# Residual written into the down projection's banks by ScalarE, in the FFNs of a four-FFN encoder trunk

## The chip, the core and the metric

The kernel runs on one NeuronCore of one Trainium2 chip. The metric is the device time of one execution in microseconds. Three runs of the kernel before took 912.9, 914.19 and 914.21 us; the median is 914.19.

## The reference

Two macaron layers over 256 tokens of width 1024, in float32. Each has an FFN, a mixer and a second FFN, and each of the three is followed by a layernorm over a scaled residual (DeepNorm). Here `ALPHA` is (2*2)^0.25, about 1.414, and `D_FF` is 2816.

```python
def swiglu(x, w_in, w_out):
    gu = x @ w_in
    g, u = gu[..., :D_FF], gu[..., D_FF:]
    return (jax.nn.silu(g) * u) @ w_out

for l in range(DEPTH):                       # DEPTH = 2
    x = layer_norm(ALPHA * x + 0.5 * swiglu(x, ffn_w_in[l, 0], ffn_w_out[l, 0]), ln_g[l, 0], ln_b[l, 0])
    y = mlstm_mixer(...) if l == 0 else window_attention(...)
    x = layer_norm(ALPHA * x + y, ln_g[l, 1], ln_b[l, 1])
    x = layer_norm(ALPHA * x + 0.5 * swiglu(x, ffn_w_in[l, 1], ffn_w_out[l, 1]), ln_g[l, 2], ln_b[l, 2])
```

A layernorm does not change if its input and the square root of its epsilon are scaled alike, so the kernel normalises 2*ALPHA*x + swiglu(x) with an epsilon four times as large.

## The kernel before

There are six stages, in this order: FFN, mLSTM, FFN, FFN, attention, FFN. They are numbered 0 to 5 in the code; the four FFNs are called FFN 1 to FFN 4 below. The 256 tokens are two tiles (t = 0, 1) of 128 tokens, kept as rows in `xt[t]` (128 x 1024) in SBUF.

**Products.** Every product of float32 numbers is three products of rounded parts (`mm3`, L617): high by high, high by low, low by high. The parts of a weight, `w_hi` and `w_lo`, are made on the chip from the loaded weight: ScalarE makes the high part by a copy of 128 x 1024, and VectorE makes the low part by a subtraction. They live in rings of ten buffers. `Weights` (L189) holds the plan of these splits.

**The order of the work.** The order on each engine's queue is the order in which the program issues it; each engine works its queue strictly in that order. Within an FFN a planner (`Paced`, L65, and `Weights.fill`, L376) decides after each issued matmul whether ScalarE and VectorE get another split now. It keeps estimates of when each engine is free: `on_tensor` (L162) adds n / 2.4 + 13.3 ns for a matmul with n columns and 109 ns for a transpose, and `on_scalar` (L157) adds 0.912 ns a column and 25 ns for an instruction. A split goes in as long as ScalarE's estimate isn't more than 300 ns ahead of TensorE's.

**An FFN.** The first 512 columns of gate and up run first; a narrow unit of 256 columns of gate and of up comes next (L1008 to L1030), and the rest is done in four blocks of 512 columns, each with seven products in place of eight (`seven`, L946). These need sums of pieces of the transposed x, `S1` to `S4`, which VectorE makes from the banks in which x was transposed (`x_sum`, L845) and which ScalarE and VectorE split in two parts (`S_hi`, `S_lo`). The hidden rows are transposed into `hT`, and the down projection follows in steps of 128 hidden columns: `down(n)` (L914) does n such steps, between the products of the next columns. The first step stands right after the narrow unit, whose two Silu (`sg`, one per token tile) and two products `hh` are issued just ahead of it:

```python
for t in range(2):
    sg = temp("sg")[:, 0:256]
    nc.scalar.activation(sg, ps[t][:, 0:256], AF.Silu)
    hh.append(temp("hh")[:, 0:256])
    nc.vector.tensor_mul(hh[t], sg, ps[t][:, 256:512])
...
down(1)
```

**The banks.** PSUM is used as two rings of four banks of 128 x 512: `pw` (`wbank`) for the products on the way, and `py` (`ybank`). The four `py` banks of an FFN are y[t][o], token tile t and half o of the 1024 output columns; they are taken at the first `down` and gather all 22 steps. Before that, the same ring holds the transposed x from which `S1` to `S4` are made.

**The tail and the layernorm.** The last six steps are done by `tail` (L716): tile 0 first, then tile 1, so that the layernorm of tile 0 lies beside the matmuls of tile 1, and that of tile 1 beside the next stage. `Norm.half` (L679) adds the scaled residual on VectorE, x <- alpha*x + y, and takes the statistics of x; `finish` (L695) makes mean and factor (the power on GpSimd), then x <- (x - mean) * g and x <- x * factor + b. `emit_x` (L766) transposes the finished x for the next stage. In the last FFN the second half of tile 1 is split: `first` (L684) adds a first part of its sum early, and two quarters of 256 columns (`quarter`, L689) are added at the very end; there the two passes of the layernorm are done in halves of 512 columns, and each half goes out by a transfer of its own.

Of the kernel before, what the change touches and what calls it, by code (L numbers as in the profile page):

```python
# [16 lines left out]
D = 1024  # L17
S = 256
DEPTH = 2
ALPHA = (2 * DEPTH) ** 0.25  # L20
LN_EPS = 1e-5
# [43 lines left out]
class Paced:  # L65
# [94 lines left out]
            self.mark(o, self.act + 125)  # L160

    def on_tensor(self, name, n, out, ins):  # L162
        self.pe = max(self.pe, self.when(*ins)) + (109.0 if name == "transpose" else n / 2.4 + 13.3)
        for o in out:
            self.mark(o, self.pe + 200)
        if self.filler is not None:
            self.filler()
# [277 lines left out]
def trunk_kernel(ctx: ExitStack, tc: tile.TileContext, x, ffn_w_in, ffn_w_out, ln_g, ln_b, ml_w_in, ml_gate_b,  # L445
                 ml_norm_g, ml_w_out, at_w_in, at_sink, at_w_out, out):
    nc = Paced(tc.nc)
# [126 lines left out]
    xt = [state.tile([128, D], F32, name=f"x{t}", tag=f"x{t}") for t in range(2)]  # L574
# [18 lines left out]
    ident = consts.tile([128, 128], F32, name="ident")  # L593
# [3 lines left out]
    mhalf = consts.tile([128, 2], F32, name="mhalf")  # L597
    nc.gpsimd.memset(mhalf, -0.5)

    gcol = consts.tile([128, 8], F32, name="gcol")  # L600
    gw = consts.tile([128, 8, 16], F32, name="gw")
    gbias = consts.tile([128, 1], F32, name="gbias")
# [14 lines left out]
    def mm3(o, l, r, start, stop, onto=False):  # L617
        nc.tensor.matmul(o, l[0], r[0], start=start, stop=False, skip_group_check=onto)
        nc.tensor.matmul(o, l[0], r[1], start=False, stop=False, skip_group_check=onto)
        nc.tensor.matmul(o, l[1], r[0], start=False, stop=stop, skip_group_check=onto)  # L620

    def pair(p, *idx):
        return p[0][idx], p[1][idx]
# [4 lines left out]
    def ybank(shape=(128, 512)):  # L628
        return psum.tile(list(shape), F32, name="py", tag="py", bufs=4)

    A = slice(None)

    def tok(t):
        return slice(t * 128, (t + 1) * 128)
# [15 lines left out]
    def to_xT(t, src, bank, halves=range(2), high=None):  # L650
        for h in halves:
            p = bank((128, 4, 128))
            for k in range(4):
                nc.tensor.transpose(p[:, k], src[:, (4 * h + k) * 128:(4 * h + k + 1) * 128], ident)
            split_evac(pair(xT, A, slice(4 * h, 4 * h + 4), tok(t)), p, high=high)
            turned[t, h] = p

    def warm(n):

        p = ybank((128, 4, 128))  # L660
        for j in range(n):
            nc.tensor.transpose(p[:, j % 4], ident, ident)

    def load_ln(room, l, n):
        t = []
# [7 lines left out]
    class Norm:  # L673
        def __init__(self, t, ca, eps, gb, last=False):
            self.t, self.ca, self.eps, self.gb, self.last = t, ca, eps, gb, last
            self.stats = state.tile([128, 44], F32, name="stats", tag="stats", bufs=2)[:, 0:18].rearrange("p (h s) -> p h s", h=3)
            self.parts = 2

        def half(self, h, y):  # L679
            z = xt[self.t][:, h * 512:(h + 1) * 512]  # L680
            nc.vector.scalar_tensor_tensor(z, z, self.ca, y, op0=OP.mult, op1=OP.add)
            nc.vector.bn_stats(self.stats[:, h], z)

        def first(self, h, y):  # L684

            z = xt[self.t][:, h * 512:(h + 1) * 512]
            nc.vector.scalar_tensor_tensor(z, z, self.ca, y, op0=OP.mult, op1=OP.add)

# [6 lines left out]
        def finish(self, spare):  # L695
            mv = state.tile([128, 2], F32, name="mv", tag="mv", bufs=2)
            nc.vector.bn_aggr(mv, self.stats[:, 0:self.parts])
            rs = state.tile([128, 2], F32, name="rs", tag="rs", bufs=2)
            nc.vector.tensor_scalar(rs[:, 0:1], mv[:, 1:2], self.eps, None, op0=OP.add)
            nc.gpsimd.tensor_tensor(rs[:, 1:2], rs[:, 0:1], mhalf[:, 0:1], op=OP.pow)  # L700
            z = xt[self.t]
            cuts = [slice(0, 512), slice(512, D)] if self.last or self.t and LC[bound[0]] else [A]
            for s_ in cuts:
                nc.vector.scalar_tensor_tensor(z[:, s_], z[:, s_], mv[:, 0:1], self.gb[0][:, s_],
                                               op0=OP.subtract, op1=OP.mult)
            if len(cuts) == 1:
                W.done(0, spare)
            for s_ in cuts:
                nc.vector.scalar_tensor_tensor(z[:, s_], z[:, s_], rs[:, 1:2], self.gb[1][:, s_],
                                               op0=OP.mult, op1=OP.add)  # L710
                if self.last:
                    nc.sync.dma_start(out[0, tok(self.t), s_], z[:, s_])
            if len(cuts) > 1:
                W.done(0, spare)

    def tail(y, h, todo, first, norm, last, turn_at, between=None, rooms_=None):  # L716

        def one(t, o, n):
            c, (i, w) = todo[t][n]
            end = n == len(todo[t]) - 1 or last and t == o == 1 and n == len(todo[t]) // 2 - 1  # L720
            mm3(y[t][o], h(c, t), pair(w, A, 0, slice(o * 512, o * 512 + 512)), first and n == 0, end)

        full = len(todo[0])
        cut = full - BACK[bound[0]]
        for o, ns in ((0, range(cut)), (1, range(cut)), (0, range(cut, full)), (1, range(cut, full))):
            for n in ns:
                if between is not None and o == 1 and n == turn_at:
                    between()
                one(0, o, n)
                if W.landed:  # L730
                    W.done(0, 0)
            if ns.stop == full and cut < full or cut == full and ns.start == 0:
                norm[0].half(o, y[0][o])
        norm[0].finish(0)
        full = len(todo[1])
        half = full // 2
        order = [(1, n) for n in range(half)] + [(0, n) for n in range(full)] + [(1, n) for n in range(half, full)]
        more = iter(RS[8 * bound[0]:8 * bound[0] + 8])
        for j, (o, n) in enumerate(order):
            if j == full + turn_at:  # L740
                emit_x(0, last)
            if last and j == full + half:
                break
            one(1, o, n)
            if last and j == half - 1:
                norm[1].first(1, y[1][1])
            if j >= half and (n < half) == (o == 0):
                W.done(todo[1][n][1][0] + 1, next(more))
            if n == full - 1:
                norm[1].half(o, y[1][o])  # L750
        if last:
            for q in range(2):
                yq = wbank((128, 256))
                for n in range(half, full):
                    c, (i, w) = todo[1][n]
                    mm3(yq, h(c, 1), pair(w, A, 0, slice(512 + 256 * q, 768 + 256 * q)), n == half, n == full - 1)
                norm[1].quarter(1, q, yq)
        norm[1].finish(1)
        if rooms_ is not None:
            norm[0].gb.clear()  # L760
            W.back(rooms_, 2)
        W.done(most=TD[bound[0]])
        W.owed, W.landed = 0, False
        return lambda: emit_x(1, last)
# [5 lines left out]
    def ffn(l, i, n, pending, last):  # L770
        with ExitStack() as ph:
# [10 lines left out]
            start = pending is None  # L782
# [7 lines left out]
            def tr(hB, t, h):  # L790
                p = wbank((128, 4, 128))
                for k in range(4):
                    nc.tensor.transpose(p[:, k], h[:, k * 128:(k + 1) * 128], ident)
                split_evac(pair(hB, A, A, tok(t)), p, wait=True)

            def chunks(hB, n_):
# [115 lines left out]
            y = []  # L912

            def down(n_):  # L914
                if not y:
                    y.extend([ybank() for _ in range(2)] for _ in range(2))
                W.flush()
                for _ in range(n_):
                    c = done_[0]
                    w, = W.take(1)  # L920
                    for t in range(2):
                        for o in range(2):
                            mm3(y[t][o], pair(hT[c], A, tok(t)), pair(w, A, 0, slice(o * 512, o * 512 + 512)),
                                c == 0, False)
                    W.done()
                    done_[0] += 1

# [105 lines left out]
            def turn():  # L1033
                p = wbank((128, 2, S))
                for t in range(2):
                    for k in range(2):
                        nc.tensor.transpose(p[:, k, tok(t)], hh[t][:, k * 128:(k + 1) * 128], ident)
                split_evac(hp, p, wait=True)

            down(1)  # L1040
# [4 lines left out]
            W.flush()  # L1045
            nc.filler = None
            W.landed = True
            norm = [Norm(t, 2 * ALPHA, 4 * LN_EPS, gb, last) for t in range(2)]
            todo = list(zip(range(2 * UNITS - 6, 2 * UNITS), W.take_rows(6)))
            W.done(0)  # L1050
            return tail(y, lambda c, t: pair(hT[c], A, tok(t)), (todo, todo), False, norm,
# [584 lines left out]
```

## Time and profile before

| | |
|---|---|
| runs | 912.9, 914.19, 914.21 us (median 914.19) |
| profiled execution, from first to last instruction (span) | 911.7 us |
| median over span (what lies around it) | 2.5 us |
| TensorE busy, matmuls | 902.5 us (99%) |
| VectorE busy | 804.4 us (88%) |
| ScalarE busy | 573.1 us (63%) |
| GpSimd busy | 152.5 us (17%) |
| mean granted TensorE clock | 0.999 |

The page gives no time of the profiled execution beside its span. PE is TensorE's matmuls, PEld its weight loads, DVE is VectorE, ACT is ScalarE, POOL is GpSimd. A matmul row has the start and the duration of one matmul, and neighbours overlap because they are pipelined. In a row in order of time the first two numbers are start and duration in microseconds, then come engine, line, operation, written tile <- read tiles, shapes and count, and in brackets how long the engine was idle before it and what ended that. In a row of a group the numbers behind the bar are busy time in microseconds, the mean of one in nanoseconds, and the engine's idle time before them. Nearly all compute instructions have L180 as their line, since a helper issues them; tile names tell them apart: `py` is a bank of y (or of a transposed x), `sg` a Silu, `S_hi` a part of an x sum, `stats` the layernorm's statistics.

### The profile page before, as it was taken

To read this page: it belongs to the slowest core of one execution; us is meant where nothing else is said; L and a number is where in the kernel's file an instruction comes from. 1 tells how busy PE (TensorE), PEld (TensorE's weight loads), DVE (VectorE), ACT (ScalarE), POOL (GpSimd) and SP (SyncE) were. 2 spreads that over 40 slices of the span, in tenths; PEclk is the share of its full clock that TensorE was granted. 3 is DMA by queue.
4 is the path that set the end of the run, shared out by engine and by line. 5 is a ranking of instruction groups with operands and counts; after the bars stand their busy time and mean duration, and the time that the engine had idled before them with its cause. 6 is when DMAs were issued, how large, how long until landed. Compare 5 with 4: busy or idle time off the path is not lost.

```text
span 911.7 us, 12563 instructions
## 1 busy us (share of the span) xinstructions
PE 902.5 (99%) x4459; PEld 757.4 (83%) x4459; DVE 804.4 (88%) x971; ACT 573.1 (63%) x793; POOL 152.5 (17%) x192
## 2 busy tenths in 40 slices
PE   9999999999999999999999999999999999999996
PEld 7888888889988888888888888888898888888885
DVE  5999999886799898999888899998869889899886
ACT  5776777356664656776646676764569566676660
POOL 0111123113211011212011111110425301111110
PEclk9999999999999999999999999999999999999999
DMA  8999998546637898997868989986534587899851
GB/s 281 367 328 259 288 274 215 162 137 186 208 111 246 296 234 244 290 285 234 241 193 269 259 257 283 272 223 197 159 119 140 163 293 221 204 298 278 252 138 47
DMA packets 100703, 208.53 MB, mean 229 GB/s; under 512 B 6904, under 2 KB 21264, under 8 KB 100640
## 3 DMA queue, kind: packets, MB, share of 16 engines
q1 hardware_dynamic: 82368, 173.04, 54.2%
q0 software_dynamic: 17696, 33.65, 22.3%
q10 hardware_dynamic: 576, 1.05, 0.3%
q8 instruction: 35, 0.57, 0.3%
q14 instruction: 28, 0.23, 0.1%
HBM read 206.65 MB, written 1.05 MB: 228 GB/s over the span
## 4 chain that ended last, share of the span: by engine, by line
PE 98%; DVE 1%; DMA 0%; issue 0%; DVEq 0%
PE pw L180 64%; PE py L180 35%; DMA x<-in_x_dram 0%; DVE x L180 0%; DVE stats L180 0%; DVEq L1632 0%; DVE mv L180 0%; DVE rs L180 0%
## 5 line engine op out<-in xcount | busy, mean ns | idle before, releaser
L180 DVE TENSOR_TENSOR w_lo<-w_raw,w_hi 128x1024 fp32r<-128x1024 f32 (+1 forms) x213 | 255.2, 1219 | 26.6 <-ACT w_hi L180 24.8
L180 ACT CAST w_hi<-w_raw 128x1024 fp32r<-128x1024 f32 (+1 forms) x213 | 218.9, 1049 | 80.3 <-PE py L180 21.7
L180 DVE TENSOR_TENSOR w_lo<-s_raw,w_hi 128x1024 fp32r<-128x1024 f32 x192 | 228.6, 1219 | 18.3 <-ACT w_hi L180 18.2
L180 ACT CAST w_hi<-s_raw 128x1024 fp32r<-128x1024 f32 x192 | 196.6, 1054 | 58.4 <-PE py L180 23.3
L180 PE MATMUL pw<-w_hi,xT_hi 128*128 128x512 f32 x480 | 189.5, 396 | 0.0
L180 PE MATMUL pw<-w_hi,xT_lo 128*128 128x512 f32 x480 | 187.0, 391 | 0.0
L180 PE MATMUL pw<-w_lo,xT_hi 128*128 128x512 f32 x480 | 186.7, 390 | 0.0
L122 POOL DMA_DIRECT2D s_raw<-in_ffn_w_in_dram x64 | 77.4, 1211 | 484.1 <-DVE s_raw L180 226.3
L180 PE MATMUL py<-w_hi,h_hi 128*128 128x512 f32 x349 | 138.2, 396 | 0.0
L180 PE MATMUL py<-w_hi,h_lo 128*128 128x512 f32 x349 | 136.2, 390 | 0.0
L180 PE MATMUL py<-w_lo,h_hi 128*128 128x512 f32 x349 | 136.0, 390 | 0.0
L180 PEld LDWEIGHTS pw<-w_hi,xT_lo 128*128 128x128 f32 x480 | 90.0, 188 | 19.1
L180 PEld LDWEIGHTS pw<-w_lo,xT_hi 128*128 128x128 f32 x480 | 90.3, 188 | 18.6 <-DVE w_lo L180 1.2
L180 PEld LDWEIGHTS pw<-w_hi,xT_hi 128*128 128x128 f32 x480 | 90.1, 188 | 17.4 <-ACT w_hi L180 0.2
L180 PE MATMUL pw<-w_hi,S_hi 128*128 128x512 f32 x256 | 99.7, 390 | 0.0
L180 PE MATMUL pw<-w_lo,S_hi 128*128 128x512 f32 x256 | 99.7, 389 | 0.0
L180 PE MATMUL pw<-w_hi,S_lo 128*128 128x512 f32 x256 | 99.7, 389 | 0.0
L180 PEld LDWEIGHTS py<-w_hi,h_lo 128*128 128x128 f32 x349 | 65.5, 188 | 14.1
L180 DVE TENSOR_TENSOR s_raw<-s_raw,s_raw 128x1024 f32<-128x1024 f32 x64 | 76.8, 1219 | 0.3
L180 PEld LDWEIGHTS py<-w_lo,h_hi 128*128 128x128 f32 x349 | 65.7, 188 | 13.0
L180 PEld LDWEIGHTS py<-w_hi,h_hi 128*128 128x128 f32 x349 | 65.6, 188 | 12.7
L180 PEld LDWEIGHTS pw<-w_hi,S_lo 128*128 128x128 f32 x256 | 48.1, 188 | 10.0
(205 smaller groups left out, 1122.7 us busy)
## 6 DMA issues: line engine op xcount, KB each, us to landing
s_raw<-in_ffn_w_in_dram SPq DMA_DIRECT2D x96, 512.0 KB, 8.0
w_raw<-in_ffn_w_out_dram SPq DMA_DIRECT2D x88, 512.0 KB, 6.1
w_raw<-in_ffn_w_in_dram SPq DMA_DIRECT2D x64, 512.0 KB, 5.7
s_raw<-in_ffn_w_in_dram POOLq DMA_DIRECT2D x64, 512.0 KB, 8.3
w_raw<-in_ml_w_in_dram SPq DMA_DIRECT2D x24, 512.0 KB, 4.6
w_raw<-in_ffn_w_in_dram SPq DMA_DIRECT2D x32, 256.0 KB, 6.0
w_raw<-in_at_w_in_dram SPq DMA_DIRECT2D x12, 512.0 KB, 4.8
w_raw<-in_ml_w_out_dram SPq DMA_DIRECT2D x8, 512.0 KB, 4.1
```

The lines of the kernel that those rows point to most:

```text
L122: self.nc.gpsimd.dma_start(ap, source, accum_op=OP.add)
L180: r = f(out, *args, **kw)
```

## The change

In the FFNs, and only there, the scaled residual is added in PSUM. When `down` takes the four y banks, ScalarE writes 2*ALPHA*x into each (four instructions of 128 x 512 per FFN), and all matmuls of the down projection add to what is there: the first step no longer starts a sum. `Norm` is made without a factor for these stages: `half` takes the statistics straight from the bank, `first` copies the early part of the last half-row from its bank to x on ScalarE, and the first pass of `finish` reads the banks, in two halves of 512 columns. The mLSTM and the attention keep the old path.

[...]

```diff
     def on_tensor(self, name, n, out, ins):
-        self.pe = max(self.pe, self.when(*ins)) + (109.0 if name == "transpose" else n / 2.4 + 13.3)
+        self.pe = max(self.pe, self.when(*ins)) + (109.0 if n == 128 else n / 2.4 + 13.3)
...
+    def turn_in(o, a, k):
+        nc.tensor.matmul(o, a, ident, is_transpose=True, start=k == 0, stop=True, skip_group_check=k > 0)
...
+            self.y = {} if ca is None else None
 
         def half(self, h, y):
+            if self.y is not None:
+                nc.vector.bn_stats(self.stats[:, h], y)
+                self.y[h] = y
+                return
...
         def first(self, h, y):
 
+            if self.y is not None:
+                nc.scalar.copy(xt[self.t][:, h * 512:(h + 1) * 512], y)
+                self.y[h] = None
+                return
...
-            for s_ in cuts:
-                nc.vector.scalar_tensor_tensor(z[:, s_], z[:, s_], mv[:, 0:1], self.gb[0][:, s_],
+            for s_ in cuts if self.y is None else [slice(0, 512), slice(512, D)]:
+                y = None if self.y is None else self.y[s_.start // 512]
+                nc.vector.scalar_tensor_tensor(z[:, s_], z[:, s_] if y is None else y, mv[:, 0:1], self.gb[0][:, s_],
                                                op0=OP.subtract, op1=OP.mult)
...
             def down(n_):
                 if not y:
                     y.extend([ybank() for _ in range(2)] for _ in range(2))
+                    for t in range(2):
+                        for o in range(2):
+                            nc.scalar.mul(y[t][o], xt[t][:, o * 512:o * 512 + 512], 2 * ALPHA)
                 W.flush()
...
                             mm3(y[t][o], pair(hT[c], A, tok(t)), pair(w, A, 0, slice(o * 512, o * 512 + 512)),
-                                c == 0, False)
+                                False, False, True)
...
-            norm = [Norm(t, 2 * ALPHA, 4 * LN_EPS, gb, last) for t in range(2)]
+            norm = [Norm(t, None, 4 * LN_EPS, gb, last) for t in range(2)]
```

More of the change, by code (lines that the diff above doesn't have):

```diff
@@ L653, in to_xT @@
             for k in range(4):
-                nc.tensor.transpose(p[:, k], src[:, (4 * h + k) * 128:(4 * h + k + 1) * 128], ident)
+                turn_in(p[:, k], src[:, (4 * h + k) * 128:(4 * h + k + 1) * 128], k)
             split_evac(pair(xT, A, slice(4 * h, 4 * h + 4), tok(t)), p, high=high)
@@ L661, in warm @@
         for j in range(n):
-            nc.tensor.transpose(p[:, j % 4], ident, ident)
+            turn_in(p[:, j % 4], ident, j % 4)
     def load_ln(room, l, n):
@@ L720, in one @@
             end = n == len(todo[t]) - 1 or last and t == o == 1 and n == len(todo[t]) // 2 - 1
-            mm3(y[t][o], h(c, t), pair(w, A, 0, slice(o * 512, o * 512 + 512)), first and n == 0, end)
+            mm3(y[t][o], h(c, t), pair(w, A, 0, slice(o * 512, o * 512 + 512)), first and n == 0, end,
+                norm[0].y is not None)
         full = len(todo[0])
@@ L792, in tr @@
                 for k in range(4):
-                    nc.tensor.transpose(p[:, k], h[:, k * 128:(k + 1) * 128], ident)
+                    turn_in(p[:, k], h[:, k * 128:(k + 1) * 128], k)
                 split_evac(pair(hB, A, A, tok(t)), p, wait=True)
@@ L1036, in turn @@
                     for k in range(2):
-                        nc.tensor.transpose(p[:, k, tok(t)], hh[t][:, k * 128:(k + 1) * 128], ident)
+                        turn_in(p[:, k, tok(t)], hh[t][:, k * 128:(k + 1) * 128], 2 * t + k)
                 split_evac(hp, p, wait=True)
```

## The prediction

> **What bounds the kernel now.** I read the page first: the share of each engine and the chain that ended last. Then the waits of TensorE, then the busy time by stage, and last the order in time on ScalarE and TensorE where the change puts its new work.
>
> ```profile
> span 911.7 us, 12563 instructions
> PE 902.5 (99%) x4459; PEld 757.4 (83%) x4459; DVE 804.4 (88%) x971; ACT 573.1 (63%) x793; POOL 152.5 (17%) x192
> ...
> PE 98%; DVE 1%; DMA 0%; issue 0%; DVEq 0%
> ```
>
> TensorE is busy for 902.5 of 911.7 us and makes up 98% of the chain. Its waits on another engine or a transfer, as matmul and as weight load, end quickly; the largest that isn't in the first microseconds of start-up:
>
> ```profile
> PEld pw L180 <- DVE w_lo L180: 1.5, 4, 0.4
> ```
>
> Busy time by stage (two halves of the FFN work, the seam between FFN 2 and FFN 3, and the end; columns: length, then TensorE, its weight loads, VectorE, ScalarE, GpSimd):
>
> ```profile
> 291.00:449.00 158.00, 158.00 (x722) 130.96 (x721) 146.62 (x151) 105.52 (x126) 20.92 (x17) 1.00 0.90 264
> 449.00:466.00 17.00, 17.00 (x83) 14.13 (x82) 13.95 (x19) 6.21 (x9) 1.46 (x1) 1.00 0.63 205
> 466.00:625.00 159.00, 158.98 (x725) 131.47 (x724) 146.78 (x152) 105.89 (x127) 20.75 (x17) 1.00 0.88 256
> 888.00:912.00 24.00, 16.67 (x84) 13.95 (x82) 14.32 (x26) 0.98 (x2) 1.85 (x2) 0.96 0.12 44
> ```
>
> The reader is to see that TensorE has no gap in an FFN, and none at the seam where the layernorm runs (17.00 of 17.00). VectorE is at 92 to 93% in the FFNs, ScalarE at 67%, but neither makes TensorE wait. So work taken from VectorE pays nothing there, while any wait put in front of a matmul lengthens the run by its full length: no slack downstream takes it up. The only stretch that TensorE doesn't cover is the last 7 us.
>
> **What is taken away.** Per FFN the four scalar_tensor_tensor of Norm.half (x <- alpha*x + y, 128x512), 16 in all (one of them in `first`, which becomes a ScalarE copy).
>
> ```profile
> L180 DVE SCALAR_TENSOR_TENSOR x<-x,py 128x512 f32<-128x512 f32 x24 | 16.4, 682 | 3.9 <-PE py L180 3.6
> L180 DVE SCALAR_TENSOR_TENSOR x<-x,mv,ln_g 128x1024 f32<-128x1024 f32 x10 | 12.8, 1276 | 0.0
> L180 DVE SCALAR_TENSOR_TENSOR x<-x,mv,ln_g 128x512 f32<-128x512 f32 x4 | 2.8, 742 | 0.0
> L180 ACT CAST S_hi<-S 128x512 fp32r<-128x512 f32 x16 | 10.0, 623 | 15.2 <-DVE S L180 15.1
> L180 ACT CAST h_hi<-pw 128x512 fp32r<-128x512 f32 x44 | 25.8, 585 | 20.6 <-PE pw L180 20.6
> ```
>
> 16 x 0.682 = 10.9 us leave VectorE. The layernorm's first pass now reads two banks of 512 in place of one row of 1024: 2 x 0.742 - 1.276 = 0.21 us more, in six layernorms (the three FFNs that are not last, two token tiles each), 1.2 us. VectorE falls by about 9.7 us to 794.7. I cost that at nothing in time, because TensorE's matmuls cover all of it; what it could give at most outside the end is the 1.5 us of waits on w_lo, if VectorE's backlog is their cause. bn_stats reads a bank instead of x; x<-x,py, which reads a bank, is no slower than the rows that don't, so no change there.
>
> The banks of y stay in use until the layernorm's first pass has read them, later than before by the statistics and one pass. The next that wants them are the transposes of the finished x into banks of the same ring, and those need the second pass anyway, so nothing is added. No queue of transfers is moved: SyncE and GpSimd issue what they did. The transposes written as matmuls with other start flags are the same instruction with the same duration: nothing. In the planner (on_tensor) only the four 64-wide transposes of the mLSTM get another estimate, 40 for 109 ns; the 16 new ScalarE writes count 492 ns each there, so that after them about 2 us of weight splits are written down later in the program. Below nothing is possible here too, by an order that happens to suit; I take zero and keep it in the range.
>
> **What is added, and where it stands.** 16 ScalarE writes, four per FFN, on the first call of `down`. Program order on ScalarE is: the two Silu of the narrow unit (L1026), then the four writes, and only then can TensorE's first down matmul (L923) start, since it accumulates on what is written. Before, this matmul needed only h and a split weight, both long there. So I look at who was first in time in each FFN. TensorE's first py matmul (in the first FFN also its fourth, which opens the second bank), then ScalarE around the Silu:
>
> ```profile
> 42.45 0.39 PE L180 MATMUL py<-w_hi,h_hi 128*128 128x512 f32 x1
> 43.13 0.39 PE L180 MATMUL py<-w_hi,h_hi 128*128 128x512 f32 x1
> ...
> 42.93 1.05 ACT L180 CAST w_hi<-w_raw 128x1024 fp32r<-128x1024 f32 x1 [2.82 <-DMA w_raw<-in_ffn_w_in_dram]
> 43.89 0.65 ACT L180 ACTIVATE sg<-pw 128x256 f32<-128x256 f32 x2
> 44.42 1.05 ACT L180 CAST w_hi<-s_raw 128x1024 fp32r<-128x1024 f32 x1
> ```
>
> ```profile
> 325.17 0.39 PE L180 MATMUL py<-w_hi,h_hi 128*128 128x512 f32 x1
> 325.61 1.05 ACT L180 CAST w_hi<-w_raw 128x1024 fp32r<-128x1024 f32 x1
> 326.57 0.65 ACT L180 ACTIVATE sg<-pw 128x256 f32<-128x256 f32 x2
> ```
>
> ```profile
> 500.87 0.39 PE L180 MATMUL py<-w_hi,h_hi 128*128 128x512 f32 x1
> 502.23 0.62 ACT L180 CAST S_hi<-S 128x512 fp32r<-128x512 f32 x1 [0.88 <-DVE S L180]
> 502.76 1.05 ACT L180 CAST w_hi<-w_raw 128x1024 fp32r<-128x1024 f32 x1
> 503.71 0.64 ACT L180 ACTIVATE sg<-pw 128x256 f32<-128x256 f32 x2
> 504.25 1.05 ACT L180 CAST w_hi<-s_raw 128x1024 fp32r<-128x1024 f32 x1
> ```
>
> ```profile
> 764.07 0.39 PE L180 MATMUL py<-w_hi,h_hi 128*128 128x512 f32 x1
> 764.52 1.05 ACT L180 CAST w_hi<-w_raw 128x1024 fp32r<-128x1024 f32 x1
> 765.47 0.64 ACT L180 ACTIVATE sg<-pw 128x256 f32<-128x256 f32 x2
> ```
>
> In all four, TensorE begins the down projection while ScalarE still has a weight split and both Silu in front of it (in FFN 3 it even waits for VectorE's S first). The new writes take the place that the next split had: 0.53 us after the start of the Silu pair (44.42 - 43.89; 504.25 - 503.71 gives 0.54).
>
> The duration of a write from SBUF into a bank is in no row. Same shape from SBUF to SBUF takes 0.623, from a bank to SBUF 0.585; I take 0.62, nearest by its source. Ends: 0.585, and 1.05 for a full 1024-wide cast as the worst. From the end of a ScalarE write to TensorE's start:
>
> ```profile
> 5.70 1.14 ACT L180 CAST w_hi<-w_raw 128x512 fp32r<-128x512 f32 x2 [0.89 <-DMA w_raw<-in_ffn_w_in_dram]
> 6.88 0.30 PEld L180 LDWEIGHTS pw<-w_hi,xT_hi 128*128 128x128 f32 x2 [0.21 <-ACT w_hi L180]
> ```
>
> 5.70 + 1.14 = 6.84, weight load at 6.88: 0.04 us. If the weight load has to wait with its matmul, half of that row's 0.30 more, so 0.04 to 0.19.
>
> So the first py matmul moves by
> - FFN 1: 44.42 + 0.62 + 0.04 - 42.45 = 2.63
> - FFN 2: 326.57 + 0.53 + 0.66 - 325.17 = 2.59
> - FFN 3: 503.71 + 0.54 + 0.66 - 500.87 = 4.04
> - FFN 4: 765.47 + 0.53 + 0.66 - 764.07 = 2.59
>
> together 11.85 us. The second to fourth bank cost nothing: a write follows the last after some 0.53 us, and TensorE spends three matmuls, 43.13 - 42.45 = 0.68 us (0.227 each), on each bank. Behind the writes on ScalarE the splits come about 4 x 0.53 = 2.1 us later, and VectorE's low parts with them; TensorE, their reader, is itself 2.6 to 4.0 us later, so they are not late for it. If that cover is gone (a split due right then), up to 2.1 us per FFN would come on top.
>
> **The end.** Last FFN, VectorE's last half-row and TensorE's last matmul:
>
> ```profile
> 902.56 0.69 DVE L180 SCALAR_TENSOR_TENSOR x<-x,py 128x512 f32<-128x512 f32 x1 [1.05 <-PE py L180]
> 903.28 0.69 DVE L180 BATCH_NORM_STATS2 stats<-x 128x6 f32<-128x512 f32 x1
> ...
> 904.71 0.42 DVE L180 TENSOR_TENSOR x<-x,pw 128x256 f32<-128x256 f32 x1
> ...
> 904.39 0.28 PE L180 MATMUL pw<-w_hi,h_lo 128*128 128x256 f32 x1
> ```
>
> The step at 902.56 goes, so VectorE gains 903.28 - 902.56 = 0.72 us. But the addition at 904.71 needs TensorE's last matmul, 904.39 + 0.28 = 904.67, which is late next. Gain between 0 and 0.72; matmul ends are modelled, so I keep both ends and take 0.05.
>
> **The sum.** Profiled execution: 911.7 + 11.85 - 0.05 = 923.5 us of span. The median of the runs, 914.19, stands 2.5 us above that span, as what lies around it: 923.5 + 2.5 = 926.0 us, 1.3% slower.
>
> [...] TensorE's granted clock after its last matmul (stage view, the column after GpSimd):
>
> ```profile
> 904.00:905.00 1.00, 0.67 (x6) 0.47 (x4) 0.96 (x3) 0.00 (x0) 0.00 (x0) 1.00 0.00 0
> ...
> 909.00:910.00 1.00, 0.00 (x0) 0.00 (x0) 0.00 (x0) 0.00 (x0) 0.00 (x0) 0.93 1.01 379
> ```
>
> It is full until about 909.86 (0.93 is 0.86 of a microsecond at 1.00 and 0.14 at 0.50), 5.2 us after the last matmul. A stall of 4.04 us is under that, so the sum has no term for a slower clock. [...]
>
> **The rivals.**
> - Shorter stalls. If the split ahead of the Silu falls elsewhere in the planner's order and VectorE's lag is less, the floor is the Silu after TensorE's own end of the unit: that ends 0.16 us after the first py matmul's old start (0.39 - 0.227), then 0.04, 0.25 to the next start on ScalarE, 0.62, 0.04: 1.1 us. FFN 1 keeps its 2.63 (nothing ahead of its first write changes), the others 1.1 each: 5.9 us, 920.1. For it: 2.6 us is mostly one split of 1.05. Against: that split stands there in all four.
> - Late splits. ScalarE's 2.1 us starve VectorE, which is at 93%, and TensorE meets missing low parts later. At the full 2.1 us in two to four FFNs: 930 to 934. Against: TensorE's own delay is larger than ScalarE's.
> - A colder clock, from the point where a stall passes the 5.2 us seen at the end: FFN 3 would have to be 1.2 us worse, and then matmuls at 0.50 take double; each microsecond so spent costs half of one, for a length no row shows: 927 to 929.
> - Faster. The end of the kernel pays the whole 0.72 us, and the writes are in the banks before TensorE arrives: 913.5. Everything they read (x) is ready long before; the one thing against is their place behind the Silu. It decides only if the four stalls together stay under 0.7 us, and each of the four orders above speaks against that.
> - That the writes are overwritten instead of added to would change the result, not the wait: the same time as forecast.
>
> **How the numbers follow.** Forecast 0.69, shorter stalls 0.13, late splits 0.10, colder clock 0.05, faster 0.02, and 0.01 that the parts cancel within 0.2% (1.8 us, about what a measurement of this kernel can tell from no change). So faster 0.02, same 0.01, slower 0.97. The forecast's own range: writes of 0.585 to 1.05 give -0.1 to +1.7 us, the weight load's 0.15 four times +0.6, the end's -0.7, and the runs shown lie from 912.9 to 914.21, so 923.9 to 928.3. Eight in ten reach from 920.5, near the shorter stalls, to 930.0, where the late splits begin.
>
> **What would show it.** After the change: four waits of TensorE on ScalarE's writes of y, of 2.6, 2.6, 4.0 and 2.6 us, and TensorE's busy time the same 902 us in a longer span; VectorE near 795 us, ScalarE near 584 (17 x 0.6 more); 16 new ScalarE rows of about 0.62 us; 8 of the 24 rows x<-x,py left; the granted clock full up to the end; the last addition still right behind the last matmul. The prediction is wrong if these waits are missing or short, if TensorE shows many small waits on w_lo instead, or if the tail after the last matmul shrinks by more than 0.7 us.

## The result, and the profile after

The changed kernel takes 928.63 us (median of four runs, 927.58 to 929.92) against 913.78 us before: ratio 1.0165, 95% interval 1.0151 to 1.018. It is 1.65% slower. The profiled execution took 928.08 us with a span of 926.4, 14.7 us more than the 911.7 of before.

The page of the changed kernel (span; busy time by engine; the chain that ended last) and, from its view of waits, what TensorE waits for as matmul and as weight load:

```profile
span 926.4 us, 12573 instructions
PE 908.5 (98%) x4459; PEld 760.9 (82%) x4459; DVE 796.4 (86%) x961; ACT 583.5 (63%) x810; POOL 145.6 (16%) x192
...
PE 87%; DVE 6%; ACT 2%; DMA 2%; issue 1%; DVEq 0%; SPq 0%; POOL 0%; ACTq 0%; POOLq 0%
...
PE py L180 <- ACT py L180: 9.1, 4, 2.6
...
PEld py L180 <- ACT py L180: 10.8, 4, 3.1
```

Four new waits of TensorE on ScalarE's writes of y have appeared, 9.1 us together. The chain, which was TensorE for 98%, now runs through VectorE, ScalarE and transfers as well, since at each of these waits it goes back to what the writes stood behind. But TensorE is also *busy* for 6.0 us longer (908.5 against 902.5) with the same 4459 matmuls. Waits alone don't do that.

The four places in order of time, TensorE's first down matmul in each FFN (the bracket is the idle time before it), and for FFN 2 ScalarE's queue and the matmuls on both sides:

```profile
41.96 0.39 PE L180 MATMUL pw<-w_hi,xT_lo 128*128 128x512 f32 x1
43.98 0.50 PE L180 MATMUL py<-w_hi,h_hi 128*128 128x512 f32 x1 [1.63 <-ACT py L180]
...
327.56 1.04 ACT L180 CAST w_hi<-w_raw 128x1024 fp32r<-128x1024 f32 x1
328.50 0.65 ACT L180 ACTIVATE sg<-pw 128x256 f32<-128x256 f32 x2
329.04 2.16 ACT L180 ACTIVATE py<-x 128x512 f32<-128x512 f32 x4
...
326.88 0.39 PE L180 MATMUL pw<-w_hi,xT_lo 128*128 128x512 f32 x1
329.70 0.71 PE L180 MATMUL py<-w_hi,h_hi 128*128 128x512 f32 x1 [2.43 <-ACT py L180]
330.21 0.63 PE L180 MATMUL py<-w_lo,h_hi 128*128 128x512 f32 x1
330.63 0.63 PE L180 MATMUL py<-w_hi,h_lo 128*128 128x512 f32 x1
...
336.88 0.39 PE L180 MATMUL pw<-w_hi,xT_hi 128*128 128x512 f32 x1
...
506.92 0.39 PE L180 MATMUL pw<-w_hi,xT_lo 128*128 128x512 f32 x1
509.94 0.50 PE L180 MATMUL py<-w_hi,h_hi 128*128 128x512 f32 x1 [2.63 <-ACT py L180]
517.10 0.39 PE L180 MATMUL pw<-w_hi,xT_hi 128*128 128x512 f32 x1
...
774.34 0.39 PE L180 MATMUL pw<-w_hi,xT_lo 128*128 128x512 f32 x1
777.14 0.80 PE L180 MATMUL py<-w_hi,h_hi 128*128 128x512 f32 x1 [2.42 <-ACT py L180]
784.20 0.39 PE L180 MATMUL pw<-w_hi,xT_hi 128*128 128x512 f32 x1
```

Against the place that each first down matmul would have had (0.227 us after the one ahead of it), the delays are 1.79, 2.59, 2.79 and 2.57 us, together 9.74. After the wait in FFN 2 the matmuls are 0.43 us apart (330.21 to 330.63) and not 0.227. The two down steps, 24 matmuls, take 336.88 - 329.70 = 7.18 us there, 7.16 in FFN 3 and 7.06 in FFN 4, where 24 x 0.227 = 5.44 would do: 1.74, 1.72 and 1.62 us more, together 5.1. 9.7 + 5.1 = 14.8, which is the 14.7 to within the rounding.

Why they are slow is in the stage view of the changed kernel (length, busy time of TensorE, weight loads, VectorE, ScalarE, GpSimd, then the granted clock; the last two columns are the transfers' busy share and GB/s):

```profile
328.00:329.00 1.00, 0.00 (x0) 0.00 (x0) 0.82 (x3) 1.00 (x3) 0.00 (x0) 1.00 1.04 270
329.00:330.00 1.00, 0.30 (x1) 0.30 (x2) 1.00 (x3) 1.00 (x3) 0.00 (x0) 0.91 1.03 342
330.00:331.00 1.00, 1.00 (x3) 0.77 (x3) 1.00 (x2) 1.00 (x3) 0.00 (x0) 0.50 1.07 393
...
333.00:334.00 1.00, 1.00 (x5) 0.77 (x5) 1.00 (x2) 0.00 (x0) 0.00 (x0) 0.89 0.46 176
...
510.00:511.00 1.00, 1.00 (x4) 0.86 (x5) 1.00 (x2) 1.00 (x3) 0.00 (x0) 0.86 1.04 393
...
776.00:777.00 1.00, 0.00 (x0) 0.00 (x0) 0.82 (x3) 1.00 (x4) 0.00 (x0) 0.98 1.05 303
```

The clock falls to 0.50 at 329.82 (0.91 is 0.82 us at full and 0.18 at half) and is back at 333.22 (0.89): 3.4 us at half rate, worth half of that. The same happens from 510.72 and from 776.96. FFN 1, with the shortest wait (1.63 us), keeps the full clock (1.00). I call such a stretch of 3.4 us a cold window below.

The tail, VectorE and then TensorE's last matmul, answers to the rows of the end of before:

```profile
917.26 0.70 DVE L180 BATCH_NORM_STATS2 stats<-py 128x6 f32<-128x512 f32 x1 [2.37 <-PE py L180]
...
919.41 0.42 DVE L180 TENSOR_TENSOR x<-x,pw 128x256 f32<-128x256 f32 x1
...
919.09 0.28 PE L180 MATMUL pw<-w_hi,h_lo 128*128 128x256 f32 x1
```

The addition that was dropped is gone, VectorE is early for the first quarter, and the last addition still starts 0.04 us after TensorE's last matmul (919.09 + 0.28 = 919.37). From there to the end it is 7.0 us, as before (911.7 - 904.71 = 7.0).

### The profile page after: what moved, and what is told of

The parts are those of the page before. It is cut to its first block, busy times and chain, and to the rows that moved or that the text cites. A ratio compares the mean times of both kernels' runs of the same rounds, so it can differ in the third digit from the quotient of the medians.

```text
span 926.4 us, 12573 instructions
## 1 busy us (share of the span) xinstructions
PE 908.5 (98%) x4459; PEld 760.9 (82%) x4459; DVE 796.4 (86%) x961; ACT 583.5 (63%) x810; POOL 145.6 (16%) x192
## 4 chain that ended last, share of the span: by engine, by line
PE 87%; DVE 6%; ACT 2%; DMA 2%; issue 1%; DVEq 0%; SPq 0%; POOL 0%; ACTq 0%; POOLq 0%
PE pw L180 52%; PE py L180 35%; DVE w_lo L180 3%; DMA w_raw<-in_ffn_w_in_dram 1%; ACT w_hi L180 1%; DMA w_raw<-in_ffn_w_out_dram 1%; DVE S L180 1%; DVE S_lo L180 1%; DVE x L180 0%; ACT sg L180 0%; DVE s_raw L180 0%; DVE hh L180 0%; ACT py L180 0%; DVE h_lo L180 0%; ACT xT_hi L180 0%
## 5 line engine op out<-in xcount | busy, mean ns | idle before, releaser
L180 PE MATMUL py<-w_hi,h_hi 128*128 128x512 f32 x349 | 140.8, 403 | 9.1 <-ACT py L180 9.1
L180 PEld LDWEIGHTS pw<-w_lo,S_hi 128*128 128x128 f32 x256 | 48.1, 188 | 10.0
```

Of the source, the lines that this page charges most:

```text
L180: r = f(out, *args, **kw)
```

## The experiments

### Is it ScalarE's extra work, or the wait?

e1_writes_aside is the kernel before with this in `down`, where the banks are taken (`aside` is a tile in SBUF that nobody reads; 1920 columns per FFN against the change's 2048):

```diff
+                    for j in range(5):
+                        nc.scalar.mul(aside, xt[j % 2][:, 0:384], 2 * ALPHA)
```

> The kernel before, with five ScalarE writes of 128x384 from x into an SBUF tile that nobody reads, at the place where the change writes the banks (1920 columns per FFN against the change's 2048). TensorE waits for none of them. Theory (wait and clock: TensorE waits for the first bank 9.7 us in all, and three of the four waits are followed by 3.4 us at half clock, 5.1 us): nothing of that can happen here, so the time is that of the kernel before, 913.8 within 1 us, no new waits of TensorE, clock 0.999. Rival (late splits: ScalarE's 2 us of extra work before the next weight splits starve TensorE later): the 5 us that the four waits don't explain stay, 917 to 919.

Measured: 914.48 us against 913.70, ratio 1.0007 (0.9998 to 1.0016). ScalarE's extra work at this place costs no more than the interval's 1.5 us. So it is not the splits behind it that come too late. The change's own trace says the same: its weight loads wait for low parts (`w_lo`) for 1.1 us in all, against 1.5 before. (In e1_writes_aside itself, where TensorE is not held up, it is 3.0 us, so the work is not quite free there.)

e2_writes_only is the kernel before with the change's four writes; the first down step keeps its start flag.

```diff
                 if not y:
                     y.extend([ybank() for _ in range(2)] for _ in range(2))
+                    for t in range(2):
+                        for o in range(2):
+                            nc.scalar.mul(y[t][o], xt[t][:, o * 512:o * 512 + 512], 2 * ALPHA)
```

> The kernel before, with only the four ScalarE writes into the banks added where the change has them; the first step of the down projection still starts its sum and so overwrites them, and the residual is added by VectorE as before. Theory (wait and clock): the write-after-write wait of TensorE is the same, so four waits of 1.8 to 2.8 us and about three cold windows, 927 to 930, as the change. Rival (taking work from VectorE pays something under the waits, or reading banks in the layernorm costs something): a difference to the changed kernel's 928.6 of more than 2 us, slower if VectorE's relief pays.

Measured: 928.06 us, ratio 1.0166 (1.0139 to 1.0194), as the change itself. So the writes ahead of the first down matmul account for the whole loss, to within the interval's 2.5 us. The single runs spread from 926.33 to 933.73. The profiled one is the slowest, and its rows show where such a spread can come from (ScalarE in FFN 1; TensorE's first down matmul in FFN 1 and FFN 3; ScalarE early in FFN 3):

```profile
44.05 1.04 ACT L180 CAST w_hi<-w_raw 128x1024 fp32r<-128x1024 f32 x1 [2.99 <-DMA w_raw<-in_ffn_w_in_dram]
...
46.20 0.79 PE L180 MATMUL py<-w_hi,h_hi 128*128 128x512 f32 x1 [3.09 <-ACT py L180]
...
515.62 0.50 PE L180 MATMUL py<-w_hi,h_hi 128*128 128x512 f32 x1 [3.69 <-ACT py L180]
...
496.01 1.05 ACT L180 CAST w_hi<-w_raw 128x1024 fp32r<-128x1024 f32 x1 [1.57 <-DMA w_raw<-in_ffn_w_out_dram]
```

In FFN 1 the split ahead of the Silu waits for a load. It could start at 41.83 in the profiled execution of the change, and only at 44.05 here, and TensorE waits 1.63 and 3.09 us. In FFN 3 TensorE waits 3.69 us where the change has 2.63. The clock adds to it: it is at half for 6.8 us in FFN 1 (45.13 to 51.96), two cold windows in a row, and for one window in each of the other three, so five windows where the change has three. The mean clock of this run is 0.989; the other three have 0.995, which fits fewer cold windows.

### Is the rest the clock?

e3_kept_busy fills the wait of the changed kernel with matmuls:

```diff
                     y.extend([ybank() for _ in range(2)] for _ in range(2))
+                    for j in range(10):
+                        nc.nc.tensor.matmul(y[1][1], xT[0][:, 0, 0:128], pieces[3][0][:, 0], start=j == 0, stop=j == 9)
```

> The changed kernel, with ten extra matmuls of 512 columns into the fourth y bank ahead of the write into it, between the narrow unit and the first down step of each FFN: some 2.3 us of TensorE work that lies inside the wait for the first bank. The result is the same, since the write replaces what they leave. Theory (wait and clock): the wait stays as a length of time, but TensorE is busy in it, so the clock stays full: 928.6 - 5.1 = 923.5 within 1 us, clock 0.999. Rival (no part of the loss is the clock; the matmuls after the wait are slow for another reason, or late splits): no gain, 928.6 or more.

Measured: 933.73 us, ratio 1.0218 (1.0204 to 1.0232), 5 us slower than the change: neither outcome. The edit did something else besides. FFN 2, TensorE and then ScalarE:

```profile
327.90 2.43 PE L932 MATMUL py<-w_hi,xT_hi 128*128 128x512 f32 x10
332.55 0.50 PE L180 MATMUL py<-w_hi,h_hi 128*128 128x512 f32 x1 [2.23 <-DVE hh L180]
...
327.81 0.62 ACT L180 CAST S_hi<-S 128x512 fp32r<-128x512 f32 x1 [0.88 <-DVE S L180]
330.41 1.04 ACT L180 CAST w_hi<-w_raw 128x1024 fp32r<-128x1024 f32 x1 [1.97 <-PE py L932]
331.36 0.65 ACT L180 ACTIVATE sg<-pw 128x256 f32<-128x256 f32 x2
```

The extra matmuls read a split weight, and ScalarE's next split waits for them ("PE py L932"). So Silu and writes start only when the extra matmuls are done, and the wait comes after them instead of beside them. (The bracket names `hh`, which ends at 332.52, about when the first write does; in FFN 3 the same wait of 2.23 us is put down to the write.) The time of this run doesn't answer the question; its trace shows something else of the clock, which stands in the last section. e5_kept_busy_free reads the transposed x instead:

```diff
+                    for j in range(10):
+                        nc.nc.tensor.matmul(y[1][1], xT[0][:, 0, 0:128], xT[0][:, 0:2], start=j == 0, stop=j == 9)
```

> As e3_kept_busy, but the ten extra matmuls read two pieces of the transposed x in place of a split weight, so that no split on ScalarE has to wait for them. Theory (wait and clock): the first down step starts when it does in the changed kernel (waits of 1.8 to 3.5, 2.6, 2.8 and 2.6 us, now filled with 2.3 us of matmuls), the clock stays full, and the 5.1 us of the cold windows are gone: 923.5 within 1.5 us, in single runs less spread than the changed kernel. Rival (the slow matmuls after the wait are not caused by TensorE's idleness): 928 or more, with half clock in the records.

Measured: 923.91 us (923.21 to 924.57), ratio 1.0109 (1.0092 to 1.0126). TensorE has 40 more matmuls to do than in the change and the kernel is 4.7 us faster. The mean clock is back at 0.998, and what is left of the waits is 0.7 us:

```profile
PE py L180 <- ACT py L180: 0.7, 3, 0.3
```

e6_part_filled does the same with four matmuls in place of ten (`range(4)`).

> As e5_kept_busy_free, but with four extra matmuls (0.9 us) in place of ten, so that TensorE is idle for some 1.7 us in each wait instead of 2.6. [...] If each idle stretch by itself, however short, made a cold window: 928. [...]

Measured: 924.18 us, ratio 1.011 (1.0094 to 1.0126), the same as with ten. FFN 2 and the stage view around it:

```profile
327.89 1.07 PE L932 MATMUL py<-xT_hi 128*128 128x512 f32 x4
330.48 0.50 PE L180 MATMUL py<-w_hi,h_hi 128*128 128x512 f32 x1 [1.52 <-ACT py L180]
...
329.00:330.00 1.00, 0.00 (x0) 0.00 (x0) 0.82 (x2) 1.00 (x4) 0.00 (x0) 1.00 1.07 281
```

TensorE is idle for 1.5 us here and for 1.5 to 1.7 in the other three FFNs, and in all four the clock stays at 1.00. So the loss of the change has two parts: the delay of the first down matmul (about 10 us, still there in both runs) and the cold windows (about 5 us, gone in both).

### Can the wait go, and what is the rest of the change worth?

e7_after_s4 issues the four writes earlier: before the narrow unit in FFN 1, and behind S4's parts in the others.

```diff
+            if start:
+                write_y()
             ps = [wbank(), wbank()]
...
                         if a == n_:
                             f_()
+                    if a == XP[3]:
+                        write_y()
```

> The changed kernel with all four writes together, placed behind S4's high part in FFN 2 to 4 (ahead of the last weight split and of both Silu) and before the narrow unit in FFN 1. Theory (wait and clock): FFN 1 has no wait; in the others the first bank is written 0.53 + 0.60 us after S4's high part starts, so TensorE waits 1.1 us each, too short for a cold window: 913.3 + 3.4 = 916.7 within 1 us, clock full. Rival (the loss comes in cold windows mainly, a short wait costs nothing): 914.

Measured: 916.95 us, ratio 1.0036 (1.0023 to 1.0049), with three waits, none in FFN 1:

```profile
PE py L180 <- ACT py L180: 3.1, 3, 1.3
```

e4_written_early takes them as far ahead as the banks' old contents allow, and does the first down step in the order in which they are written. `put(t, o)` is one write; in FFN 2 to 4 `first_y` stands between S2's subtraction and its high part, `more_y` between S4's addition and its high part, and `put(0, 1)` behind that; in FFN 1 all four stand before the narrow unit:

```diff
+            def first_y():
+                y.extend(([ybank()], []))
+                put(0, 0)
+
+            def more_y():
+                y[0].append(ybank())
+                y[1].extend(ybank() for _ in range(2))
+                put(1, 0)
+                put(1, 1)
...
+                    for t, o in ((0, 0), (1, 0), (1, 1), (0, 1)) if c == 0 else ((0, 0), (0, 1), (1, 0), (1, 1)):
```

> The changed kernel with the same four writes per FFN moved ahead: in the first FFN before the narrow unit, in the others y[0][0] right after VectorE's S2 has read its old content, the two banks of tile 1 after S4's, and y[0][1] last, with the first down step in that order of banks. Theory (wait and clock): the banks are written before TensorE arrives, no wait, no cold window, and since the tail after the last matmul is not shorter either: 914 within 1 us. Rival (late splits, or S parts that come later, take the wait's place): 916 to 920 with new waits of TensorE on w_lo or S_lo. Rival (the rest of the change is worth something by itself): under 912.5.

Measured: 913.25 us against 913.70, ratio 0.9994 (0.9985 to 1.0003): no difference to the kernel before that the interval would show, and 15 us less than the change. FFN 2, ScalarE and then TensorE:

```profile
320.40 0.60 ACT L180 ACTIVATE py<-x 128x512 f32<-128x512 f32 x1
...
324.05 1.12 ACT L180 ACTIVATE py<-x 128x512 f32<-128x512 f32 x2
325.10 0.61 ACT L180 CAST S_hi<-S 128x512 fp32r<-128x512 f32 x1
325.61 0.60 ACT L180 ACTIVATE py<-x 128x512 f32<-128x512 f32 x1
326.14 1.04 ACT L180 CAST w_hi<-w_raw 128x1024 fp32r<-128x1024 f32 x1
327.08 0.64 ACT L180 ACTIVATE sg<-pw 128x256 f32<-128x256 f32 x2
...
325.12 0.39 PE L180 MATMUL py<-w_hi,h_hi 128*128 128x512 f32 x1
```

The first bank is ready 4 us before TensorE's first down matmul, and the others in time for theirs: no wait of TensorE on a write of y is left. The Silu start 1.96 us after that matmul where it was 1.40 before, at no measurable cost. The writes fill time in which ScalarE waited for VectorE's sums. VectorE is 8.8 us less busy here too (795.6 against 804.4), and that buys nothing that can be measured; no matmul was waiting for it.

## Why the prediction was right or wrong

The forecast was 926.0 us, range 920.5 to 930.0, slower with 0.97. Measured: 928.6. Direction and range held, and four waits on the writes are the mechanism that was forecast, but a third of the loss has another cause, and the size is right only by luck: two errors of opposite sign partly cancel. The waits came out 2.1 us shorter than the 11.85 that were summed, and the cold windows added 5.1 us that stood in no term. With the waits as forecast, the cold windows would have made it about 926.0 + 5.1 = 931.1 us, outside the range.

- **TensorE has no slack, so a wait counts in full.** Right. 9.7 us of delays and 5.1 us of cold windows give 14.8 of the measured 14.7 us.
- **VectorE's 10 us less pay nothing.** Right for the time as a whole, shown by e4_written_early. VectorE came to 796.4 us (forecast 794.7), ScalarE to 583.5 (584).
- **The wait in FFN 2 and FFN 4.** Right: 2.59 and 2.57 us against 2.59 and 2.59. A write into a bank took 0.599 us where 0.62 was taken, and the group starts 0.54 us after the Silu.
- **The wait in FFN 1**, 2.63 us. Too long by 0.84: 1.79. This term rests on when a load lands, since the split ahead of the Silu waits for it. That load varies from execution to execution: the split's start is 42.93 in the profile of before, 41.83 in the change, 44.05 in e2_writes_only. One trace can't give this term better than within a microsecond or more.
- **The wait in FFN 3**, 4.04 us. Too long by 1.25: 2.79. It was read from a queue that stood behind VectorE's sum S4. The run with the writes but the old layernorm has 3.69 us of wait there, close to the forecast, and the change 2.63. FFN 3 is the only one that follows another FFN, whose layernorms VectorE now does with less work. It is no accident of one trace: counted from the place that TensorE's first down matmul would have had, the Silu start after 2.8, 2.7 and 2.7 us in the three traces with the old layernorm (before, e1_writes_aside, e2_writes_only), and after 1.6, 1.5 and 1.6 in three with the new one and the writes in the same place (the change, e5_kept_busy_free, e6_part_filled). So the sentence that VectorE's relief is worth nothing failed in this one place: it goes with a shorter new wait. How it gets there (loads of down weights that land earlier: the split in front waits 1.57 us for one in e2_writes_only) is argued from the rows, and no run isolates it.
- **The clock.** This step failed. It took the 5.2 us from the last matmul to the fall of the clock at the end of the trace as the least that a wait must last, and so gave the sum no term, and the rival "a colder clock" a chance of 0.05. The change shows cold windows after TensorE was idle for 2.43, 2.63 and 2.42 us; its mean clock is 0.993 and TensorE's busy time 908.5 us, where a full clock and the same 902 were to be seen. Nor are the 5.2 us a fixed length: at the end of the change the clock falls at 923.74 (0.87 from 923 to 924), 4.4 us after the last matmul (919.37). The falls in the change, at 329.82, 510.72, 776.96 and 923.74, lie 180.90, 266.24 and 146.78 us apart, which is 53.0, 78.0 and 43.0 times 3.413 us, and each cold window lasts 3.4 us. So an estimate from these figures is a grid of 3.413 us on which the changes of the clock lie in this execution, wherever the waits end. Counted back in such steps from the fall at 909.86, the end of before has a stretch without a matmul (906.45 to 909.86) and ahead of it one in which TensorE is busy for 1.63 us (903.04 to 906.45); the clock is 1.00 in both. The 5.2 us are the idle rest of the one, 1.8, and the whole of the other.
- **The end.** Right: nothing gained, since the last addition waits for TensorE.
- **Banks read by the layernorm, start flags, planner.** Costed at nothing, and nothing by e4_written_early as a whole. The transposes that `turn_in` now issues take as long as before: the median is 272 ns before and after for those of `hh`, 273 and 272 ns for those of `x`. What their other start flags do for the adding was not shown, since the change was not run without them.

Of the rivals, "late splits" is refuted by e1_writes_aside, "faster" by the four waits. "Shorter stalls" did not happen as it was put: FFN 2 and FFN 4 kept their 2.6 us, and of the two waits that were about a microsecond shorter one is FFN 1, which that rival left as it was. "A colder clock" came true besides the forecast, with waits of about half the 5.2 us that it asked for.

## What to carry to other kernels

Where an engine has no gap, read a change by what the engine's next instruction will newly wait for, and by what stands ahead of the producer in its own queue; here a write of 0.6 us cost 2.6 us, because one weight split and two Silu were in front. Where the producer has idle time earlier and its operands are ready, issue it there: the same writes moved a few microseconds ahead cost nothing. And a wait of TensorE may be paid twice: nine of the ten waits of 2.23 us or more in these traces were followed by half clock, and none of those up to 1.73 us. It was 3.4 us at half clock nearly each time, some 1.7 us more. A few matmuls whose result is thrown away, inside the wait, avoided that (the clock is 1.00 in e6_part_filled), once nothing else had to wait for what they read.

## What the runs showed of the hardware that was not expected

- In the change half clock came without an idle stretch as long as a cold window. The 3.41 us ahead of the three falls in the change's FFNs are 326.41 to 329.82, 507.31 to 510.72 and 773.55 to 776.96. By the starts and ends in the rows, TensorE is busy in them for 0.98, 0.78 and 1.18 us, the idle times (2.43 in the first, for instance) taken off: 29, 23 and 35%. In e2_writes_only the clock falls after 3.41 us that are busy for 1.44, 42% (779.00 to 782.41). At the end of the kernel before it stays after 3.41 us with 1.63, 48% (903.04 to 906.45). In e6_part_filled, where it stays in all four FFNs, TensorE is idle for 1.73 us at most, so 3.41 us around one wait are busy for 1.68 or more, 49%, wherever they begin. A limit between 42 and 48% is an estimate from these figures alone, as far as the modelled ends of the matmuls can be trusted. The two stretches, of e2_writes_only and of before, columns as above:

```profile
779.00:782.41 3.41, 1.44 (x7) 0.86 (x5) 3.23 (x5) 2.53 (x6) 0.00 (x0) 1.00 1.04 244
...
903.04:906.45 3.41, 1.63 (x14) 1.43 (x12) 3.24 (x9) 0.00 (x0) 0.26 (x1) 1.00 0.00 0
```

- The length of a wait alone did not decide. In e3_kept_busy TensorE waits for the same 2.23 us in FFN 2, FFN 3 and FFN 4. In FFN 2 and FFN 4 the clock falls to 0.50, at 333.21 and 783.77, and the 3.41 us ahead of the fall are busy for 35 and 41%. In FFN 3 the clock stays at 1.00. In steps of 3.413 us from the fall in FFN 2 (an estimate from the distances in the change; the two falls here are 450.56 us apart, 132.0 steps) the wait in FFN 3 lies across two stretches, busy for 51 and 84%. Whether one kernel differs in this from execution to execution was not shown: the mean clocks of e2_writes_only, 0.989 and 0.995, would fit one, the four runs of the change, 0.992 to 0.993, show none. The three stretches of e3_kept_busy, in this order of FFNs:

```profile
329.80:333.21 3.41, 1.18 (x6) 0.67 (x5) 1.44 (x3) 2.80 (x6) 0.00 (x0) 1.00 1.05 389
510.71:514.12 3.41, 1.73 (x8) 1.12 (x6) 1.48 (x3) 1.77 (x5) 0.00 (x0) 1.00 1.05 375
780.36:783.77 3.41, 1.41 (x6) 1.20 (x7) 2.20 (x4) 3.41 (x7) 0.00 (x0) 1.00 1.01 387
```
- One cold window was followed by another. In FFN 1 of e2_writes_only the clock stays at half behind a stretch in which TensorE, at half clock, is busy for 2.35 us, 69%:

```profile
45.13:48.55 3.42, 2.35 (x6) 1.87 (x7) 3.02 (x4) 3.42 (x7) 0.00 (x0) 0.50 1.04 386
```

- A ScalarE write from SBUF into a bank took 0.599 us for 128x512, between the two rows from which it was estimated, 0.585 and 0.623. VectorE's pass with the operand in a bank took 742 ns, as from SBUF, and the statistics 695 ns in both cases:

```profile
L180 ACT ACTIVATE py<-x 128x512 f32<-128x512 f32 x16 | 8.6, 599 | 0.0
...
L180 DVE SCALAR_TENSOR_TENSOR x<-py,mv,ln_g 128x512 f32<-128x512 f32 x15 | 10.5, 742 | 0.0
L180 DVE BATCH_NORM_STATS2 stats<-py 128x6 f32<-128x512 f32 x15 | 10.4, 695 | 7.0 <-PE py L180 6.7
```
